# A planned kernel for a hybrid encoder: two-tensor work taken off GpSimd, and twelve planning rounds in place of one

## The chip, the cores and the metric

The kernel runs on one core of one Trainium2 chip. The time is that of the device, in microseconds (us), for the whole program from the inputs in the chip's memory to the output there. Five engines work side by side, each in the order in which its own instructions stand: TensorE (PE, matrix products; PEld is its loading of weights), VectorE (DVE), ScalarE (ACT), GpSimd (POOL), and SyncE (SP), which here only issues transfers. They wait for each other by semaphores.

## The reference

Four residual layers on a sequence of 256 tokens of 1024 numbers; layers 0 and 3 mix tokens by RWKV-7, layer 1 by stick-breaking attention, layer 2 by attention over 64 selected keys. An FFN follows each.

```python
for i in range(DEPTH):                       # DEPTH = 4
    kind, j = i % 3, i // 3
    h = rms_norm(x, norm_mix[i])
    if kind == 0:   y, v_layer = rwkv7_time_mix(h, v_first, ...)
    elif kind == 1: y = stick_breaking_attention(h, sb_w_qkv[j], sb_w_out[j])
    else:           y = dsa_attention(h, ds_w_in[j], ...)
    x = x + y
    x = x + swiglu(rms_norm(x, norm_ffn[i]), ffn_w_gu[i], ffn_w_down[i])

def rms_norm(x, g): return x * rsqrt(mean(x * x) + 1e-6) * g
def swiglu(h, w_gu, w_down):
    g, u = split(h @ w_gu, 2)
    return (silu(g) * u) @ w_down
...
# dsa_attention, for a block of 64 queries
idx = einsum('bqhd,bsd->bqhs', qi_b, ki)
score = einsum('bqh,bqhs->bqs', wi_b, relu(idx))
top_val, top_idx = lax.top_k(where(visible, score, -inf), 64)
p = softmax(q_b . k[top_idx] * 64 ** -0.5)
```

RWKV's recurrence keeps a 64 by 64 state for each of 16 heads and goes through the tokens in order; the kernel does it in four chunks of 64 tokens.

## The kernel before, in words

Everything lies with the 1024 channels on partitions (8 groups of 128) and the 256 tokens along the free axis. Weights come from memory in 397 pieces of 128 x 1024 numbers (tile raw, four slots). Where float32 accuracy is wanted at a faster matmul rate, a piece is split into a rounded part wh (an ACT or DVE copy) and its remainder wl (DVE), three slots each; activations are split the same way (xg, h, yhl, ohl, rhl).

The kernel is not issued as it is written. Each call is recorded (Plan.record) as an operation with its estimated cost and its dependencies, and Plan.schedule then builds one order for each engine: a list scheduler (_schedule) goes through the operations by rank, the length of the longest chain behind them. Some operations may go to either of two engines; the table ALTS lists them, and the scheduler picks. For "any tensor_tensor" the two were DVE and GpSimd. Where it expects PE to have nothing ready or to run too empty, it puts in matmuls of a constant (tile warm_o, two at a time), called warm-ups here.

Three kinds of storage are shared out by the plan: PSUM banks (groups ps with 5 and g with 2), SBUF slots (t with 12, wh, wl, and the big ones by name: SB, QC, PR, s0, s1, s6, s7, xb), and the groups raw and xm, which are given during scheduling in a fixed turn. For the first two kinds, _prepare walked the buffers by their first use in the order in which the program was written, gave each the slot that was last used longest ago in that order, and made every first user of the new buffer wait for all users of the old one. Ranks were computed on those dependencies. The scheduler tries a reserve of free raw slots from 1 to 6 and takes the first with which it gets through.

The parts that the prediction speaks of, by tile names:

- prep_chunk: after each quarter of a residual update (xt), its squares (sq, by ACT) are summed into sqa ("any" tensor_tensor), and xg, the scaled input of the next FFN or attention, is made (ACT and DVE).
- rwkv: kp, rp and vp are the products with plain float32 weights; lora_in, la and lw the small ones; sc the chunk scores (to SB); a triangular inverse goes through memory (scr, xa, xi, scx, XT) and is put together by cmb; then two chains of small products (xu, qu, pS, Y) go through the four chunks for each half of the heads; post makes ysd and yhl of them (two "any" tensor_tensor calls for each pair of heads), and po is the output product.
- dsa: idx are the index scores, sbt holds their weighted sum, from which 8 rounds of max and match_replace pick 64 keys for each query; mk is the mask made of it; vps the value products; then for each of 8 pairs of heads qk, its norm (qss), its rotation (qrot, with one "any" tensor_tensor), the scores z, the softmax (prs), its transpose pT, attn_o, and at the end po.
- ffn: 22 gate, 22 up and 8 down products (gate, up, dn), in split form.

Of the kernel before, what the change touches and what calls it, by code (L numbers as in the profile page):

```python
# [61 lines left out]
class Region:  # L62


    def __init__(self, p0, p1, cols, width):
        self.p0, self.p1 = p0, p1
        cols = np.asarray(cols).ravel()
        self.lo, self.hi = int(cols.min()), int(cols.max()) + 1
        self.mask = None
        if len(cols) < self.hi - self.lo or len(np.unique(cols)) < self.hi - self.lo:  # L70
            self.mask = np.zeros(width, bool)
            self.mask[cols] = True
# [106 lines left out]
class Op:  # L179


    def __init__(self, eng):
        self.eng, self.instrs, self.cost, self.table, self.cols = eng, [], 0.0, None, 0.0
        self.preds, self.succs, self.alts, self.warmer, self.parts = set(), [], {}, False, False
        self.bufs, self.ns = [], 0.0


class Queue:
# [5 lines left out]
    def __getattr__(self, method):  # L194
# [4 lines left out]
          AF.Tanh: "sigmoid_and_others", AF.Silu: "silu_and_others"}  # L199

ALTS = {("any", "copy"): [("scalar", "copy"), ("vector", "tensor_copy")],
        ("any", "tensor_tensor"): [("vector", "tensor_tensor"), ("gpsimd", "tensor_tensor")],
        ("any", "memset"): [("gpsimd", "memset"), ("vector", "memset")]}


# [10 lines left out]
ROW = 3  # L216
GAP = 1100.0
RESERVES = (1, 2, 3, 4, 5, 6)

WAIT = {"tensor": 85.0, "vector": 55.0, "scalar": 40.0, "gpsimd": 40.0, "sync": 0.0}  # L220
FREE = ("raw", "xm")
# [58 lines left out]
class Plan:  # L280
# [95 lines left out]

    def _prepare(self, counts):

        for b in self.bufs:
            if b.ops:  # L380
                b.ops = list(dict.fromkeys(b.ops))
                b.first, b.last = min(o.idx for o in b.ops), max(o.idx for o in b.ops)
        self.grouped, held = {}, {}
        for b in sorted((b for b in self.bufs if b.ops and b.group is not None), key=lambda b: b.first):
            if b.group in FREE:
                self.grouped.setdefault(b.group, []).append(b)
                for o in b.ops:
                    o.bufs.append(b)
                continue
            slots = held.setdefault(b.group, [None] * counts.get(b.group, 1))  # L390
            k = min(range(len(slots)), key=lambda i: -1 if slots[i] is None else slots[i].last)
            old = slots[k]
            if old is not None:
                assert old.last < b.first, (b.name, old.name, b.group)
                for o in b.roots:
                    o.preds |= {q for q, _ in old.writes + old.reads if q is not o}
            slots[k], b.slot = b, f"{b.group}_{k}"
        load, table, now, before = None, None, [], []
        for o in list(self.ops):
            if o.table is None:  # L400
                continue
            if o.table != table:
                table, before, now = o.table, now, []
                load = Op("scalar")
                load.cost, load.table, load.idx = 1290.0, table, o.idx - 0.5
                load.preds |= set(before)
                self.ops.append(load)
            o.preds.add(load)
            now.append(o)
        self.ops.sort(key=lambda o: o.idx)  # L410
        for o in self.ops:
            o.preds.discard(o)
            for q in o.preds:
                assert q.idx < o.idx
                q.succs.append(o)
        for o in reversed(self.ops):
            o.base = o.eng, o.cost
            o.rank = o.cost + max((s.rank + self._lat(o, s) for s in o.succs), default=0.0)

    def _schedule(self, counts, reserve):  # L420
        engines = ("tensor", "vector", "scalar", "gpsimd", "sync")
# [206 lines left out]
        return max(free.values()), sorted(out, key=lambda o: o.start)  # L628

    def schedule(self, counts):  # L630
        self._prepare(counts)
        best = None
        for reserve in RESERVES:
            r = self._schedule(counts, reserve)
            if r is not None:
                best = r
                break
        self.time, self.out = best
        Plan.last = self
        return self.out  # L640

# [1087 lines left out]
```

## Time and profile before

| | |
|---|---|
| three runs | 1474.48, 1473.09, 1474.14 us; median 1474.14 |
| profiled execution | 1473.95 us, of which the span from first to last instruction is 1472.2 |
| granted TensorE clock | 0.999 over the span |
| ACT, POOL busy | 718.3 us, 61.3 us |
| weights and other transfers | 224.55 MB, 151 GB/s read and written over the span |

The profile gives, for an engine and a kind of operation, the number of instructions, their busy time, and the mean of one, and what ended the idle time in front of them. An operation is named by what it writes and reads, without buffer numbers. Nearly all instructions are issued by one line of the planner (L661), so tiles tell them apart and lines do not. A plain float32 matmul of the program stands in the trace as two rows. The duration of a matmul reaches from issue to result, and matmuls overlap: what one costs is the distance from one start to the next. The stages, by time: RWKV 13 to 225 us, FFN to 406, stick-breaking to 530, FFN to 711, sparse attention to 882, FFN to 1064, RWKV to 1285, FFN to the end.

### The profile page before, as it was taken

The page shows a single profiled execution, that of the slowest core. Times are in us where ns is not written, and L with a number is a line of the kernel's source. Part 1 is how long each engine was busy: PE and PEld are TensorE (multiplying, and loading weights), DVE is VectorE, ACT ScalarE, POOL GpSimd, SP SyncE. Part 2 cuts the span into 40 slices and gives each one's busy share as a digit, 9 for nine tenths or more (in the row PEclk, how much of TensorE's full clock was granted, in tenths as well). Part 3 has the DMA queues.
Part 4 walks back from the last instruction along what each step waited for, and adds up shares of the span by engine and source line. Part 5 has one row for each costly group of instructions (what it writes and reads, how often), then busy time and mean ns, then how long its engine had stood idle before and what let it go on. Part 6 is the DMA issues. An engine that isn't in the chain of part 4 may idle for free.

```text
span 1472.2 us, 26233 instructions
## 1 busy us (share of the span) xinstructions
PE 1447.0 (98%) x10434; PEld 1228.1 (83%) x10434; DVE 1107.1 (75%) x2026; ACT 718.3 (49%) x1348; POOL 61.3 (4%) x57
## 2 busy tenths in 40 slices
PE   9999999999999999999999989999999999999998
PEld 6788788888888888888977868888877877888887
DVE  7297478998566779986789978986474884789864
ACT  2344665444447655444546755444325256654442
POOL 0000010000000010000100010000100001200000
PEclk9999999999999999999999999999999999999999
DMA  7234135655554445555634445555523430455653
GB/s 254 91 107 144 36 101 172 194 183 194 175 183 136 130 158 186 198 187 181 192 113 130 129 144 172 186 193 183 197 93 108 129 101 18 130 175 182 196 188 132
DMA packets 77803, 224.55 MB, mean 153 GB/s; under 512 B 23536, under 2 KB 23792, under 8 KB 77424
## 3 DMA queue, kind: packets, MB, share of 16 engines
q1 hardware_dynamic: 77680, 222.87, 46.4%
q8 instruction: 82, 1.34, 0.4%
q14 instruction: 41, 0.34, 0.1%
HBM read 219.70 MB, written 3.15 MB: 151 GB/s over the span
## 4 chain that ended last, share of the span: by engine, by line
PE 86%; DVE 9%; ACT 2%; DMA 2%; issue 1%; SPq 0%; POOL 0%; DVEq 0%
PE up L661 17%; PE dn L661 16%; PE gate L661 16%; PE qk L661 5%; PE po L661 4%; PE kp L661 4%; PE rp L661 4%; PE vps L661 3%; PE z L661 2%; DVE wl L661 2%; PE vp L661 2%; PE warm_o L1564 1%; PE Y L661 1%; PE sc L661 1%; DVE xg L661 1%
## 5 line engine op out<-in xcount | busy, mean ns | idle before, releaser
L661 ACT CAST wh<-raw 128x1024 fp32r<-128x1024 f32 x317 | 329.7, 1050 | 401.8 <-PE dn L661 130.2
L661 DVE TENSOR_TENSOR wl<-raw,wh 128x1024 fp32r<-128x1024 f32 x349 | 420.3, 1222 | 70.0 <-ACT wh L661 58.5
L661 PE MATMUL gate<-xg,wh 128*128 128x512 f32 x704 | 259.9, 398 | 3.9 <-DVE xg L661 2.1
L661 PE MATMUL up<-xg,wh 128*128 128x512 f32 x704 | 259.9, 397 | 0.0
L661 PE MATMUL dn<-h,wh 128*128 128x512 f32 x704 | 247.6, 394 | 0.0
L661 PE MATMUL dn<-h,wl 128*128 128x256 f32 x704 | 197.5, 280 | 0.0
L661 PE MATMUL gate<-xg,wl 128*128 128x256 f32 x704 | 197.2, 280 | 0.0
L661 PE MATMUL up<-xg,wl 128*128 128x256 f32 x704 | 197.2, 280 | 0.0
L661 PEld LDWEIGHTS gate<-xg,wh 128*128 128x128 f32 x704 | 132.2, 188 | 38.1 <-DVE xg L661 3.4
L661 PEld LDWEIGHTS up<-xg,wh 128*128 128x128 f32 x704 | 132.2, 188 | 31.1
L661 PEld LDWEIGHTS dn<-h,wh 128*128 128x128 f32 x704 | 132.4, 188 | 30.8
L661 PEld LDWEIGHTS up<-xg,wl 128*128 128x128 f32 x704 | 132.8, 189 | 0.2
L661 PEld LDWEIGHTS gate<-xg,wl 128*128 128x128 f32 x704 | 132.8, 189 | 0.1
L661 PEld LDWEIGHTS dn<-h,wl 128*128 128x128 f32 x704 | 132.4, 188 | 0.0
L661 PE MATMUL qk<-xg,wh 128*128 128x256 f32 (+1 forms) x384 | 95.0, 326 | 0.1
L661 PE MATMUL qk<-xg,wl 128*128 128x256 f32 x256 | 72.0, 281 | 0.4 <-DVE wl L661 0.4
L661 PEld LDWEIGHTS qk<-xg,wh 128*128 128x128 f32 x384 | 64.2, 189 | 7.8 <-issue 1.4
L661 PE MATMUL kp<-pre,raw 128*128 128x256 f32 x256 | 59.9, 386 | 1.7 <-DVE pre L661 1.7
L661 DVE TENSOR_TENSOR gus<-gus,rstd 128x512 f32<-128x512 f32 x88 | 59.8, 687 | 1.2
L661 PE MATMUL vp<-xv,raw 128*128 128x256 f32 x256 | 59.0, 385 | 0.9 <-DVE vf L661 0.9
L661 PE MATMUL rp<-xr,raw 128*128 128x256 f32 x256 | 58.7, 382 | 0.0
L661 PEld LDWEIGHTS kp<-pre,raw 128*128 128x128 f32 x256 | 47.3, 190 | 13.3 <-issue 4.0
(292 smaller groups left out, 2355.5 us busy)
## 6 DMA issues: line engine op xcount, KB each, us to landing
raw<-in_wts_dram SPq DMA_DIRECT2D x397, 512.0 KB, 3.6
lora<-in_lora_dram SPq DMA_DIRECT2D x2, 1536.0 KB, 9.2
lg<-in_lora_dram SPq DMA_DIRECT2D x4, 512.0 KB, 5.4
xt<-in_xT_dram SPq DMA_DIRECT2D x4, 256.0 KB, 4.0
lora<-in_lora_dram SPq DMA_DIRECT2D x2, 512.0 KB, 5.6
xi<-in_id_dram SPq DMA_DIRECT2D x2, 512.0 KB, 8.0
scr<-SB SPq DMA_DIRECT2D x8, 128.0 KB, 3.4
xa<-scr SPq DMA_DIRECT2D x2, 512.0 KB, 3.3
```

The costliest lines, as they stand in the source:

```text
L661: getattr(getattr(nc, o.eng), method)(*map(real, args), **{k: real(a) for k, a in kw.items()})
L1564: lambda: [nc.tensor.matmul(wo[:, :S], wx[:, :P], wx, start=True, stop=True) for _ in range(WARMERS)])
```

## The change

Two things are changed in the planner; the computation is the same.

First, "any tensor_tensor" has only DVE left. POOL keeps some memsets and copies.

Second, slots are given anew in each of twelve rounds. _prepare now only collects the buffers and keeps each operation's own dependencies (needs). _place takes an order, sorts the buffers by their first use in that order, gives each the slot whose last user ends earliest in it, adds the waits that follow, and recomputes the ranks; the turn of raw and xm is sorted by the same order. schedule begins with the written order, schedules, and hands the outcome (without warm-ups) to the next round as its order. The round that ends earliest by the plan's own estimate is kept, with its engines, forms and slots.

```diff
 ALTS = {("any", "copy"): [("scalar", "copy"), ("vector", "tensor_copy")],
-        ("any", "tensor_tensor"): [("vector", "tensor_tensor"), ("gpsimd", "tensor_tensor")],
+        ("any", "tensor_tensor"): [("vector", "tensor_tensor")],
         ("any", "memset"): [("gpsimd", "memset"), ("vector", "memset")]}
...
+ROUNDS = 12
...
-        self.grouped, held = {}, {}
-        for b in sorted((b for b in self.bufs if b.ops and b.group is not None), key=lambda b: b.first):
...
-            slots = held.setdefault(b.group, [None] * counts.get(b.group, 1))
-            k = min(range(len(slots)), key=lambda i: -1 if slots[i] is None else slots[i].last)
-            old = slots[k]
-            if old is not None:
-                assert old.last < b.first, (b.name, old.name, b.group)
-                for o in b.roots:
-                    o.preds |= {q for q, _ in old.writes + old.reads if q is not o}
-            slots[k], b.slot = b, f"{b.group}_{k}"
...
+    def _place(self, counts, order):
+
+        at = {o: i for i, o in enumerate(order)}
+        for o in self.ops:
+            o.preds, o.succs = set(o.needs), []
+        for g, bufs in self.grouped.items():
+            bufs.sort(key=lambda b: min(at[o] for o in b.ops))
+        for g, bufs in self.placed.items():
+            slots = [None] * counts.get(g, 1)
+            for b in sorted(bufs, key=lambda b: min(at[o] for o in b.ops)):
+                k = min(range(len(slots)), key=lambda i: -1.0 if slots[i] is None else max(o.end for o in slots[i].ops))
+                old = slots[k]
+                if old is not None:
+                    for o in b.roots:
+                        o.preds |= {q for q, _ in old.writes + old.reads if q is not o}
+                slots[k], b.slot = b, f"{g}_{k}"
...
     def schedule(self, counts):
+
+
         self._prepare(counts)
-        best = None
-        for reserve in RESERVES:
-            r = self._schedule(counts, reserve)
-            if r is not None:
-                best = r
-                break
-        self.time, self.out = best
+        order, best = self.ops, None
+        for o in order:
+            o.start, o.end = o.idx, o.idx + 0.5
+        for _ in range(ROUNDS):
+            self._place(counts, order)
+            for reserve in RESERVES:
+                r = self._schedule(counts, reserve)
+                if r is not None:
+                    break
+            if best is None or r[0] < best[0]:
+                best = r + ([(o.eng, o.cost, o.instrs, o.start, o.end) for o in r[1]], [b.slot for b in self.bufs])
+            order = [o for o in r[1] if not o.warmer]
+        self.time, self.out = best[:2]
...
```

In the built programs the change shows as follows. PE has the same matmuls in another order, and 246 warm-ups in place of 294. POOL's two-tensor operations, 40 of them, stand on DVE. A few operations that may go to ACT or DVE have changed sides (so wh: 29 on DVE in place of 32). SP issues the same transfers, the weight pieces in the order in which the plan uses them.

More of the change, by code (lines that the diff above doesn't have):

```diff
@@ L184, in __init__ @@
         self.preds, self.succs, self.alts, self.warmer, self.parts = set(), [], {}, False, False
-        self.bufs, self.ns = [], 0.0
+        self.bufs, self.ns, self.end = [], 0.0, 0.0
 class Queue:
@@ L377, in _prepare @@
     def _prepare(self, counts):
+        self.grouped, self.placed = {}, {}
         for b in self.bufs:
@@ L382, in _prepare @@
                 b.first, b.last = min(o.idx for o in b.ops), max(o.idx for o in b.ops)
-        self.grouped, held = {}, {}
-        for b in sorted((b for b in self.bufs if b.ops and b.group is not None), key=lambda b: b.first):
[L385 to L389, printed above, removed]
-            slots = held.setdefault(b.group, [None] * counts.get(b.group, 1))
-            k = min(range(len(slots)), key=lambda i: -1 if slots[i] is None else slots[i].last)
-            old = slots[k]
-            if old is not None:
-                assert old.last < b.first, (b.name, old.name, b.group)
-                for o in b.roots:
-                    o.preds |= {q for q, _ in old.writes + old.reads if q is not o}
-            slots[k], b.slot = b, f"{b.group}_{k}"
+                if b.group in FREE:
+                    self.grouped.setdefault(b.group, []).append(b)
+                    for o in b.ops:
+                        o.bufs.append(b)
+                elif b.group is not None:
+                    self.placed.setdefault(b.group, []).append(b)
         load, table, now, before = None, None, [], []
@@ L412, in _prepare @@
             o.preds.discard(o)
+            o.needs, o.base = frozenset(o.preds), (o.eng, o.cost)
+    def _place(self, counts, order):
[13 more added lines that the diff above has]
+                slots[k], b.slot = b, f"{g}_{k}"
+        for o in self.ops:
+            o.preds.discard(o)
             for q in o.preds:
-                assert q.idx < o.idx
+                assert at[q] < at[o]
                 q.succs.append(o)
-        for o in reversed(self.ops):
-            o.base = o.eng, o.cost
-            o.rank = o.cost + max((s.rank + self._lat(o, s) for s in o.succs), default=0.0)
+        for o in reversed(order):
+            o.rank = o.base[1] + max((s.rank + self._lat(o, s) for s in o.succs), default=0.0)
     def _schedule(self, counts, reserve):
@@ L631, in schedule @@
         self._prepare(counts)
-        best = None
-        for reserve in RESERVES:
-            r = self._schedule(counts, reserve)
-            if r is not None:
-                best = r
-                break
-        self.time, self.out = best
+        order, best = self.ops, None
[11 more added lines that the diff above has]
+        self.time, self.out = best[:2]
+        for o, state in zip(best[1], best[2]):
+            o.eng, o.cost, o.instrs, o.start, o.end = state
+        for b, slot in zip(self.bufs, best[3]):
+            b.slot = slot
         Plan.last = self
```

## The prediction

> **What bounds the kernel now.** I read the page's shares first, then the busy time by stage, then the waits and the timeline of the places that the stages pointed to.
>
> ```profile
> span 1472.2 us, 26233 instructions
> PE 1447.0 (98%) x10434; PEld 1228.1 (83%) x10434; DVE 1107.1 (75%) x2026; ACT 718.3 (49%) x1348; POOL 61.3 (4%) x57
> PEclk9999999999999999999999999999999999999999
> PE 86%; DVE 9%; ACT 2%; DMA 2%; issue 1%; SPq 0%; POOL 0%; DVEq 0%
> ```
>
> TensorE is busy for 98% of the span at a full granted clock, and 86% of the chain that ended last is PE's. So 1472.2 - 1447.0 = 25.2 us of PE idleness is all that an order can gain, plus whatever PE does that is not work: the 294 warm-up matmuls. The busy time by stage says where the idleness lies (columns: us, then busy us of PE, PEld, DVE, ACT, POOL, granted clock, DMA share, GB/s).
>
> ```profile
> 13.00:225.00 212.00, 207.95 (x2088) 167.08 (x2088) 144.23 (x352) 100.71 (x273) 12.82 (x13) 1.00 0.35 113
> 225.00:406.00 181.00, 181.00 (x1032) 157.94 (x1031) 145.63 (x214) 83.75 (x105) 3.67 (x3) 1.00 0.55 183
> 711.00:882.00 171.00, 162.46 (x1172) 139.04 (x1171) 145.43 (x289) 101.39 (x225) 12.42 (x10) 1.00 0.44 140
> 1064.00:1285.00 221.00, 216.11 (x2158) 173.03 (x2155) 151.54 (x383) 105.92 (x280) 11.85 (x11) 1.00 0.32 99
> ```
>
> These are the first RWKV layer (4.05 us idle), an FFN (none), the sparse-attention layer (8.54) and the second RWKV layer (4.89). An FFN has nothing to give: no order makes its matmuls shorter. The three mixers hold 17.5 of the 25.2 us.
>
> **The warm-up matmuls.** The planner writes them where it expects PE to wait, so their number in a built program says how much waiting it sees. Their price is a spacing, not the 273 ns that one takes from issue to result:
>
> ```profile
> 9.21 3.88 PE L1564 MATMUL warm_o<-warm_x 128*128 128x256 bf16 x34
> L1564 PE MATMUL warm_o<-warm_x x294: 272/273/421, 1.2 to 1242.3; 128*128 128x256 bf16 x147
> ```
>
> 34 of them span 3.88 us, so (3.88 - 0.27) / 33 = 0.109 us each. The changed program's instruction list has 246: 90 instead of 96 by the end of the first RWKV layer, 36 instead of 64 in sparse attention, 86 instead of 100 for the second RWKV layer with its start, and 34 the same elsewhere. All other PE instructions are the same in kind and number, only in another order. 48 x 0.109 = **5.2 us** is gone from PE if the waits that they stood for are covered by work; if they are not, nothing is gained here (the far end, 0).
>
> **Sparse attention, its end.** Of those 28, more than all come out of the last heads: 40 warm-ups stood there (8, 6, 22 and 4), and the new list has none behind its last 8, since the products of the output projection (po) and of the last heads stand between the steps of a head. What the warm-ups didn't cover was idle:
>
> ```profile
> 829.00:870.00 41.00, 37.96 (x288) 30.52 (x288) 29.31 (x65) 25.36 (x67) 0.00 (x0) 1.00 0.39 133
> 853.34 0.73 PE L661 MATMUL qss<-rhl,bonesr 128*128 128x512 f32 x2 [0.86 <-ACT prs L661]
> 861.42 2.56 PE L1564 MATMUL warm_o<-warm_x 128*128 128x256 bf16 x22
> 864.99 0.85 PE L661 MATMUL pT<-consts,prs 128*128 128x128 f32 x6 [1.00 <-DVE prs L661]
> ```
>
> 41.00 - 37.96 = 3.0 us, each wait right behind a run of warm-ups or at a softmax step. With work in their place I take 2.0 of it as gained (bounds 0 and 3.0).
>
> **Sparse attention, its middle.** Here the change takes cover away. The selection of keys is one line of DVE work, and the masked scores wait for its end. Before, the value products (vps) stood behind the index scores; now 48 of them stand ahead of the last index scores, and 28 + 8 warm-ups (before 14 + 8) fill part of the hole.
>
> ```profile
> L661 DVE TENSOR_TENSOR wl<-raw,wh 128x1024 fp32r<-128x1024 f32 x349 | 420.3, 1222 | 70.0 <-ACT wh L661 58.5
> 747.00:776.00 29.00, 25.36 (x186) 21.10 (x186) 27.81 (x83) 13.44 (x22) 1.59 (x3) 1.00 0.26 82
> 750.91 1.58 PE L661 MATMUL idx<-ki,sbt 64*128 64x128 f32 x16
> 750.94 4.70 DVE L661 SCALAR_TENSOR_TENSOR sbt<-sbt,wi 128x256 f32<-128x256 f32 x14
> 758.26 0.08 DVE L661 MATCH_VALUE_LOAD sbt<-m,sbt 128x8 f32 x1
> 759.43 0.08 DVE L661 MATCH_VALUE_LOAD sbt<-m,sbt 128x8 f32 x1
> 761.53 0.86 DVE L661 SCALAR_TENSOR_TENSOR qa<-qa,vecs,sbt 128x256 f32<-128x256 f32 x2
> 770.06 0.67 DVE L661 TENSOR_TENSOR qa<-qrot,sbt 128x512 f32<-128x512 f32 x1
> 765.82 0.49 PE L661 MATMUL qrot<-rhl,rotr 128*128 128x512 f32 x1 [1.73 <-DVE rhl L661]
> 773.82 0.35 DVE L661 TENSOR_SCALAR mk<-sbt 128x384 bf16<-128x384 f32 x1
> 415.56 10.98 PE vps L661 x48
> 502.97 5.76 PE po L661 x48
> ```
>
> One round of the selection is 759.43 - 758.26 = 1.17 us, eight are 9.4. The new DVE list has between the last index scores and the mask (mk) 12 weighted sums (4.70 / 14 = 0.336 each, 4.0), the 9.4, four qa scalings (1.7), two weight residuals wl (1.22 each, 2.4), nine 512-wide operations of rhl, qa and qk at 0.67 (6.0) and the mask (0.4): 23.9 us. PE has 120 matmuls of qk in that stretch, at the spacing of po, whose shape is the same (5.76 / 48 = 0.12: 14.4), ten of qss and qrot (at the 0.23 of vps, 2.3), four score matmuls, half of what eight idx ones take (16 trace rows, 1.58: 0.8), and 36 warm-ups (3.9): 21.4. It will wait some 2.5 us. Before, it was idle for 29.00 - 25.36 = 3.64 in the same place. I take no difference (bounds 3.6 gained and 4 lost).
>
> **What moves from POOL to DVE.** Forty two-tensor operations: 18 + 2 sums of squares, 3 + 1 in the rotary steps (all 512 wide) and 16 of the RWKV output (256 wide). On DVE one costs what its like costs there:
>
> ```profile
> L661 DVE TENSOR_TENSOR gus<-gus,rstd 128x512 f32<-128x512 f32 x88 | 59.8, 687 | 1.2
> L661 DVE TENSOR_TENSOR ysd<-Y,ysd 128x256 f32<-128x256 f32 x16 | 6.5, 419 | 6.6 <-ACT ysd L661 6.6
> L661 POOL TENSOR_TENSOR sqa<-sqa,sq 128x512 f32<-128x512 f32 x18 | 28.7, 1595 | 555.3 <-ACT sq L661 490.8 <-issue 64.5
> L661 DVE SCALAR_TENSOR_TENSOR xg<-xt,vecs,xg 128x256 fp32r<-128x256 f32 x48 | 34.7, 759 | 0.0
> L661 DVE SCALAR_TENSOR_TENSOR xg<-xt,vecs,xg x8: 473/480/1522, 522.2 to 530.6; 128x256 fp32r<-128x256 f32 x8
> L661 DVE TENSOR_TENSOR yhl<-ysd,yhl 128x256 fp32r<-128x256 f32 x16 | 8.6, 547 | 2.3 <-ACT yhl L661 2.3
> PEld gate L661 <- DVE xg L661: 3.4, 4, 0.8
> ```
>
> 24 x 0.687 + 16 x 0.419 = 23.2 us more on DVE. But POOL's work was not free for DVE: an xg operation takes 480 ns at the median and up to 1522 beside a POOL sum, and the mean of all 48 is 759, so 48 x 0.279 = 13.4 us of DVE's busy time was waiting for POOL; yhl adds 16 x (0.547 - 0.419) = 2.0. DVE's net load is about +8 us on 1107, and where it falls DVE has slack against PE (145 of 181 us in an FFN). [...]
>
> On PE's path this touches the four passages from a mixer to an FFN, where the first gate products wait for xg in four places of up to 0.8 us (3.4 in all), and the last output heads of RWKV. In the new DVE list one sum stands ahead of the last xt addition there (0.69 later), with a wl and that addition queued behind it on DVE, and the gate products behind those; its square comes from ACT one xt addition earlier, so I see no wait in front of it. The stalled xg that followed is free again (up to 1.0 earlier). In RWKV's output the two operations behind a head's scale become 0.42 each on DVE instead of 0.7 to 1.6 on POOL. I take 1.5 us gained in all (bounds: 4 x 0.69 = 2.8 lost, the 3.4 gained).
>
> **The sum.** The profiled execution took 1473.95 us, 1.75 beside its span; the median of the runs is 1474.14. 1473.95 - 5.2 - 2.0 + 0 - 1.5 = **1465.2**. The unpriced part is where each RWKV layer's instructions, now with other banks and slots and the first weight piece pair issued ahead of the lora piece on SP, wait for each other; its 4.05 + 4.89 = 8.9 us of idleness may fall away or double. I take it unchanged.
>
> **Rivals.** (1) *The waits stay and only the filler goes.* A warm-up that is deleted from a wait which is still there saves nothing. For it speaks that 17.5 us of waiting in the mixers came on top of all warm-ups, so the planner sees too few waits; against it, that in the sparse-attention end real products replace them. Then only the 1.5 remains: 1472.5, no change. (2) *The selection becomes the bound, and the kernel is slower.* The 48 value products are 10.98 us of cover that is gone from behind the index scores. DVE serves its line in order; if the two wl in it come late, the qk products that need them stop as well, and PE waits out the cover that left, 2.5 + 11.0 instead of 2.5, so 1465.2 + 11.0 = 1476.2, and with the 1.5 not gained, 1477.7. It decides from the point where DVE's 23.9 us stretch by more than PE's own waiting hides. For it: DVE is busy for 27.81 of 29.00 us there already. Against it: of the DVE line's 23.9 us, PE has 21.4 of its own. (3) *TensorE's clock drops where warm-ups were taken out.* Before the clock is up, a warm-up takes more:
>
> ```profile
> 1.19 5.73 PE L1564 MATMUL warm_o<-warm_x 128*128 128x256 bf16 x30 [1.19 <-DVE eps_rms L661]
> ```
>
> (5.73 - 0.27) / 29 = 0.188 us against 0.109, so a cold stretch costs about 0.7 of its length again. If 10 us of the two RWKV chains, where 20 warm-ups go, ran cold, that is +7: 1472, no change. The clock row, all nines, says that nothing was near that before. [...] (4) *RWKV's own waits go too*: with 8.9 us less, 1456.
>
> **How the numbers follow.** Forecast 0.63, rival 4 0.08 (both faster), rival 1 0.13, rival 3 0.04 (both no change, which is what within 0.2%, 2.9 us, can't be told from), rival 2 0.12 (slower). So faster 0.71, same 0.17, slower 0.12. Predicted: 1465 us. Low end: the sum with 3.0, 3.6 and 3.4 gained is 1473.95 - 5.2 - 10.0 = 1458.8, and half of RWKV's idleness less gives 1454. High end: 1477, which leaves out rival 2's far end alone. The forecast's own range is 1458 to 1471.
>
> **What would show it.** Warm-ups x246; PE idle in the sparse-attention stage near 6 us instead of 8.5, and its length near 166 us; no wait over 0.5 us at its last heads; waits for the mask or rhl of about 2.5 us in its middle; xg's mean near 480 ns with no 1500 among them; POOL under 15 us busy; FFN stages still 181 us; granted clock 1.00 throughout. Wrong would be: a wait on mk, rhl or wl in the middle of 6 us or more (rival 2), stages of unchanged length with fewer warm-ups in them (rival 1), a clock under 0.99 in an RWKV stage (rival 3), or RWKV's stages growing by more than their warm-ups shrink.

## The result, and the profile after

The changed kernel takes 1455.15 us (median of four runs, 1454.46 to 1456.18) against 1473.66 for the kernel before beside it: a ratio of 0.987 (0.9856 to 0.9885), 18.5 us less. The forecast was 1465; the range of 1454 to 1477 holds the time, but the gain is twice what was forecast, and the total is that of rival 4 (1456), by luck, as shown below. The profiled execution took 1456.18 us with a span of 1454.4, so 17.8 us are to be accounted for against the 1472.2 of before.

The changed kernel's page, its shares:

```profile
span 1454.4 us, 26104 instructions
PE 1435.8 (99%) x10386; PEld 1222.8 (84%) x10386; DVE 1101.0 (76%) x2063; ACT 720.9 (50%) x1351; POOL 8.9 (1%) x17
PE 90%; DVE 6%; ACT 1%; issue 1%; DMA 1%; SPq 0%; DVEq 0%; POOL 0%
```

PE's idleness is 1454.4 - 1435.8 = 18.6 us, 6.6 less than before; its busy time is 11.2 us less, with the same real matmuls. So the larger part of the gain came out of time that the page had called busy. The warm-ups are a part of that; their rows, before and after:

```profile
L1564 PE MATMUL warm_o<-warm_x 128*128 128x256 bf16 x294 | 44.0, 285 | 1.2 <-DVE eps_rms L661 1.2
L1589 PE MATMUL warm_o<-warm_x 128*128 128x256 bf16 x246 | 36.2, 286 | 1.2 <-DVE eps_rms L686 1.2
```

They are 7.8 us less. These rows overlap their neighbours at both ends, so 48 spacings of 0.109 us, 5.2, are the low estimate. Between 3.4 and 6.0 us of the 11.2 came out of matmuls that do work.

The mixers, cut from the first working matmul of one stage to that of the next (every cut lies 0.24 us ahead of it). First the kernel before (columns as in the prediction: us; busy of PE, PEld, DVE, ACT, POOL; clock; DMA):

```profile
13.73:219.17 205.44, 202.88 (x2062) 163.24 (x2062) 137.92 (x343) 96.89 (x266) 10.31 (x11) 1.00 0.35 111
712.25:875.94 163.69, 156.02 (x1139) 133.89 (x1137) 138.60 (x281) 97.43 (x217) 9.68 (x8) 1.00 0.43 138
1070.68:1280.52 209.84, 206.84 (x2096) 165.87 (x2096) 143.96 (x370) 99.27 (x268) 9.95 (x10) 1.00 0.31 93
```

And after:

```profile
13.65:215.71 202.06, 201.01 (x2054) 161.40 (x2055) 137.57 (x352) 97.28 (x267) 2.74 (x2) 1.00 0.35 112
707.24:862.51 155.27, 150.53 (x1110) 131.11 (x1108) 128.23 (x275) 103.14 (x230) 0.29 (x2) 1.00 0.45 145
1056.93:1264.02 207.09, 204.40 (x2081) 164.76 (x2082) 144.64 (x382) 98.76 (x266) 1.13 (x1) 0.99 0.31 94
```

Sparse attention is 8.4 us shorter, the RWKV layers 3.4 and 2.7 (2.75 from unrounded starts). The idle time of PE in the three goes from 2.56, 7.67 and 3.00 to 1.05, 4.74 and 2.69: 4.75 us less, where the stages shrank by 14.55. All stages, by the same cuts (gate/up and down are the FFN's two parts), for the changed kernel and the experiments that matter most, each against the kernel before:

| stage | before, us | after | e2: one round | e3: POOL allowed | e8: slots only | e7: banks only |
|---|---|---|---|---|---|---|
| RWKV 1 | 205.44 | -3.39 | -0.06 | -2.10 | -1.74 | +1.47 |
| gate/up | 123.91 | -0.65 | -0.61 | -0.01 | -0.61 | -0.61 |
| stick-breaking | 118.48 | -0.24 | -0.45 | +0.09 | -0.45 | -0.24 |
| gate/up | 123.18 | -0.66 | -0.70 | -0.01 | -0.70 | -0.66 |
| sparse attention | 163.68 | -8.41 | -3.91 | -7.31 | -3.96 | -9.96 |
| gate/up | 123.23 | -0.11 | -0.65 | +0.55 | -0.66 | -0.66 |
| RWKV 2 | 209.83 | -2.75 | -1.51 | +0.40 | -1.56 | +4.48 |
| gate/up | 123.37 | -1.19 | -0.67 | -0.18 | -0.76 | -0.75 |
| start, the four downs, norm | | -0.36 | -0.14 | +0.10 | +0.05 | +0.35 |

In the row RWKV 2 the changed kernel, e3 and e7 ran in part at a lower clock (0.99, 0.98 and 0.97 over that stage), so it does not show their order alone. A second profile of the changed kernel gives -3.64, -8.39 and -1.81 for the three mixers.

The changed kernel's groups of instructions, and its warm-ups by their tile:

```profile
L686 PE MATMUL gate<-xg,wh 128*128 128x512 f32 x704 | 259.0, 397 | 1.6 <-DVE xt L686 1.6
L686 DVE SCALAR_TENSOR_TENSOR xg<-xt,vecs,xg 128x256 fp32r<-128x256 f32 x48 | 21.2, 478 | 0.0
L686 DVE TENSOR_TENSOR sqa<-sqa,sq 128x512 f32<-128x512 f32 x18 | 12.3, 683 | 0.0
```

```profile
L1589 PE MATMUL warm_o<-warm_x x246: 272/273/421, 1.2 to 1230.4; 128*128 128x256 bf16 x123
```

xg's mean is 478 ns (759 before, with sums on POOL); what idle time is left ahead of the gate products (1.6 us) is put down to xt, none to xg.

The middle of sparse attention, on PE's timeline after:

```profile
767.78 1.58 PE L686 MATMUL idx<-ki,sbt 64*128 64x128 f32 x16
...
778.89 3.23 PE L1589 MATMUL warm_o<-warm_x 128*128 128x256 bf16 x28
783.22 0.51 PE L686 MATMUL qrot<-rhl,rotr 128*128 128x512 f32 x1 [0.87 <-DVE rhl L686]
790.33 1.05 PE L1589 MATMUL warm_o<-warm_x 128*128 128x256 bf16 x8
792.62 0.50 PE L686 MATMUL qss<-rhl,bonesr 128*128 128x512 f32 x1 [1.01 <-DVE rhl L686]
793.05 0.93 PE L686 MATMUL z<-qk 64*128 64x128 f32 x8
```

All 36 warm-ups of the stage are these 28 + 8, and the waits behind them are 1.88 us. The masked scores z come right after the second of them: the selection of keys did not become the bound.

### The profile page after: what moved, and what is told of

Its sections match the earlier page's. It is cut to its first block, busy times and chain, and to the rows that moved or that the text cites. A ratio compares the mean times of both kernels' runs of the same rounds, so it can differ in the third digit from the quotient of the medians.

```text
span 1454.4 us, 26104 instructions
## 1 busy us (share of the span) xinstructions
PE 1435.8 (99%) x10386; PEld 1222.8 (84%) x10386; DVE 1101.0 (76%) x2063; ACT 720.9 (50%) x1351; POOL 8.9 (1%) x17
## 4 chain that ended last, share of the span: by engine, by line
PE 90%; DVE 6%; ACT 1%; issue 1%; DMA 1%; SPq 0%; DVEq 0%; POOL 0%
PE up L686 17%; PE gate L686 17%; PE dn L686 17%; PE qk L686 5%; PE po L686 5%; PE vp L686 4%; PE rp L686 4%; PE kp L686 4%; PE vps L686 3%; PE z L686 2%; PE Y L686 1%; PE sc L686 1%; DVE wl L686 1%; PE warm_o L1589 1%; PE qi L686 1%
## 5 line engine op out<-in xcount | busy, mean ns | idle before, releaser
L686 ACT CAST wh<-raw 128x1024 fp32r<-128x1024 f32 x320 | 333.9, 1050 | 412.1 <-PE dn L686 130.3
L686 PE MATMUL kp<-pre,raw 128*128 128x256 f32 x256 | 63.4, 389 | 1.9 <-DVE pre L686 1.7
```

The source lines that it names most:

```text
L686: getattr(getattr(nc, o.eng), method)(*map(real, args), **{k: real(a) for k, a in kw.items()})
```

## The experiments

The differences of the stages above tell two theories apart. The lock theory: POOL's two-tensor work blocked DVE, and its removal is the gain. The order theory: the gain is from slots given by use, round after round.

Each ratio below is against the kernel before beside it. The intervals of e4, e5, e6, e8, e11 and e12 overlap with that of the changed kernel (0.9856 to 0.9885), so between those kernels the stages of the profiled executions carry the argument, not the totals.

**e1: the order of before, POOL's 40 operations on DVE at their places.**

```diff
+eng = "vector" if o.eng == "gpsimd" and method == "tensor_tensor" else o.eng
-getattr(getattr(nc, o.eng), method)(...)
+getattr(getattr(nc, eng), method)(...)
```

> The order of the kernel before, every bank, slot and warm-up as it was; only the 40 two-tensor operations that stood on POOL are issued on DVE at the same place. Lock theory (half of the 18.5 us and more came from DVE no longer waiting for POOL): 1474 - 9 = 1465 us or less, and the four passages to an FFN give 2 to 3 us of it. Order theory (the gain came from the slots given anew, twelve times): 1471 to 1475 us, since DVE's busy time changes by only some 8 us and PE's order is fixed.

Measured: 1471.53 us (12 runs), ratio 0.998 (0.9959 to 0.9994). In the profile the four passages into gate/up gain 0.43, 0.40, 0.37 and 0.51; sparse attention gains 1.41; the first RWKV layer loses 1.40. That profiled execution is 3.6 us above its own median, with a granted clock of 0.66 from 1170 to 1180 us, so the +3.13 of its second RWKV layer is not charged to the edit. Freed from POOL but kept in the old order, the kernel gains some 3.5 us (0.9 to 6.0 by the interval).

**e2: the change with one planning round. e3: the change with POOL allowed again for two-tensor work.**

```diff
-ROUNDS = 12
+ROUNDS = 1
```

> The changed kernel with one planning round in place of twelve: no two-tensor work on POOL, slots by the written order, 332 warm-ups. Lock theory: near 1463 us. Order theory: no better than before; 38 warm-ups more than before are 4.1 us at 0.109, so 1474 to 1478 us. If warm-ups stand for nothing but waits that would be there anyway, it comes out like e1.

```diff
-        ("any", "tensor_tensor"): [("vector", "tensor_tensor")],
+        ("any", "tensor_tensor"): [("vector", "tensor_tensor"), ("gpsimd", "tensor_tensor")],
```

> Twelve rounds with POOL still allowed for two-tensor work: 46 of them on POOL, 236 warm-ups (10 fewer than the changed kernel). Order theory: as fast as the changed kernel or up to 1 us faster, 1454 to 1456 us. Lock theory: DVE is blocked by POOL for some 20 us again, and 1462 to 1466 us.

Measured: e2 1465.38, ratio 0.993 (0.9904 to 0.9949); e3 1464.60, ratio 0.992 (0.9897 to 0.9942). The spans are 8.7 and 8.5 us shorter than before, 17.2 together, against 17.8 for the whole change: two halves that add, and neither theory alone. By their totals both lie at or near what the lock theory had put down for them (1463, and 1462 to 1466); that theory fails at e1, which it put at 1465 or less, and at the places. The places differ: e2 has every passage into gate/up and 3.9 us of sparse attention, e3 none of the passages and 7.3 us of sparse attention. e2 has 332 warm-ups, 38 more than before, and is faster all the same: its first RWKV layer has 80 in place of 62 and is as long (-0.06).

**e4: the changed kernel's order, its 22 sums of squares on POOL.**

```diff
+eng = "gpsimd" if method == "tensor_tensor" and args[0].buf.name in ("sqa", "sq") \
+    and args[1].buf.name in ("sqa", "sq") else o.eng
```

> The changed kernel's order with 22 sums of squares (sqa and sq) put back on POOL at the same place. It prices the lock alone at the passages to an FFN. Lock theory: the four passages lose the 0.7 to 1.2 us each that they gained, and the total is 1458 to 1461 us. Order theory: within 1.5 us of the changed kernel, 1455 to 1456.5 us.

Measured: 1460.87, ratio 0.990 (0.9871 to 0.9921); the span is 1459.7, so the 22 sums cost 5.3 us. Its groups:

```profile
L687 DVE SCALAR_TENSOR_TENSOR xg<-xt,vecs,xg 128x256 fp32r<-128x256 f32 x48 | 34.7, 758 | 0.0
L687 POOL TENSOR_TENSOR sqa<-sqa,sq 128x512 f32<-128x512 f32 x18 | 29.4, 1631 | 841.6 <-ACT sq L687 477.2 <-issue 364.4
```

And its waits of the weight loads of PE:

```profile
PEld gate L687 <- DVE xg L687: 3.4, 4, 0.8
```

These are the kernel before's 759 ns and 3.4 us back again. Against the changed kernel the four gate/up parts grow by 0.64, 0.66, 0.83 and 0.65, 2.8 us; another 1.24 is the start, where POOL takes 2.61 us for two sums that DVE does in 1.49 (PE's ss waits 1.4 us for them, 0.55 in the changed kernel), and the rest small pieces of the mixers. By what POOL holds DVE up, no run shows: the rows show how long xg takes with a sum on POOL beside it and without. Nor does it pay here to hand two-tensor work back to GpSimd, with VectorE busy for 76% of the changed kernel's span: e3 has 46 operations on POOL, and its span is 9.3 us longer.

**e5 and e6: the changed kernel's order with one and with three matmuls for each warm-up pair, 123 and 369 in place of 246.**

```diff
-for _ in range(WARMERS)
+for _ in range(WARMERS - 1)        # e6: WARMERS + 1
```

> The changed kernel's order with one matmul in place of two wherever a warm-up stands: 123 warm-ups of 246. 50 of those left out lie at the start and before the second RWKV layer, where PE waits for the norm anyhow. Price theory (each of the other 73 costs its 0.109 us): 8 us less, 1447 us. Filler theory (they stand in waits that stay): 1453 to 1456 us with more PE idle. Clock theory: over 1456 us with a granted clock under 0.995.

> The same order with three matmuls in place of two at each warm-up: 369. Price theory: 8 us more, 1463 us, since 73 of the 123 added ones lie in the mixers at 0.109. Filler theory: 1455 to 1458 us, with PE idle shrinking by what the warm-ups grow.

Measured: e5 1462.22, ratio 0.990 (0.9864 to 0.9928); e6 1463.60, ratio 0.990 (0.9873 to 0.9933). The spans of their profiled executions are 4.0 and 6.7 us longer than the changed kernel's. Windows of e5, sparse attention and ten microseconds of the second RWKV layer:

```profile
708.09:863.38 155.29, 149.89 (x1092) 130.73 (x1091) 128.26 (x275) 103.20 (x230) 0.29 (x2) 0.99 0.46 144
...
1208.00:1218.00 10.00, 10.00 (x175) 7.91 (x174) 3.45 (x13) 4.71 (x18) 0.00 (x0) 0.52 0.08 32
```

and of e6, sparse attention and the first RWKV layer:

```profile
711.33:866.60 155.27, 151.93 (x1128) 132.78 (x1126) 128.25 (x275) 103.18 (x230) 0.29 (x2) 1.00 0.46 144
...
15.57:219.77 204.20, 203.52 (x2086) 164.23 (x2085) 137.13 (x350) 97.41 (x267) 2.90 (x2) 1.00 0.35 106
```

With 18, 36 and 54 warm-ups the stage has the same length, 155.29, 155.27 and 155.27: there a warm-up only turns idle time into busy time (5.40, 4.74, 3.34 us idle). In the first RWKV layer, 28 more make 204.20 - 202.06 = 2.14 us, 0.076 each. Neither place pays the 0.109 of the forecast. e6's total is the price theory's 1463, but by luck: the three mixers hold 3.8 of its 6.7 us (2.14, 0.00 and, for the second RWKV layer, 208.78 - 207.09 = 1.69), where that theory had 8, and most of the rest lies at the start and ahead of the second RWKV layer, which it took as free. The filler theory's total (1455 to 1458) missed as well. e5 came out as the clock theory said: what it saves in filler it loses to the clock, 0.52 in the ten microseconds shown, 0.993 over its span; its first RWKV layer begins 3.0 us later, and its second takes 3.05 us longer.

**e7 and e8: twelve rounds, but only the PSUM banks, or only the SBUF slots, given by the use in the order ahead.** The other kind is given by the order in which the program was written.

```diff
+            use = g in ("ps", "g")              # e8: g not in ("ps", "g")
-            for b in sorted(bufs, key=lambda b: min(at[o] for o in b.ops)):
-                k = min(..., key=lambda i: ... max(o.end for o in slots[i].ops))
+            for b in sorted(bufs, key=lambda b: min(at[o] for o in b.ops) if use else b.first):
+                k = min(..., key=lambda i: ... max(o.end for o in slots[i].ops) if use else slots[i].last)
```

> Twelve rounds in which only the PSUM banks (groups ps and g) are given by the use in the order ahead; SBUF slots stay as in one round. 270 warm-ups. If the gain of the rounds (10 us between one round, 1465.4, and the changed kernel, 1455.2) comes from banks: 1455 to 1459 us, with the sparse-attention stage at 155 to 157. If from SBUF slots: 1462 to 1466 us.

> The other half: only SBUF slots are given by use, the banks stay as in one round. 304 warm-ups. If the gain comes from banks: 1462 to 1466 us, sparse attention near 160. If from slots: 1455 to 1459 us.

Measured: e7 1467.02 (11 runs, 1461.66 to 1473.23), ratio 0.993 (0.9902 to 0.9952); e8 1463.90, ratio 0.990 (0.9872 to 0.9931). e7's total lies above both ranges put down for it; its runs go from 1461.66 us at a granted clock of 0.999 to 1473.23 at 0.991. The stages say more than the totals: sparse attention is 153.73 us in e7 and 159.72 in e8, against 159.78 with one round. So the rounds' gain there is the banks' alone. The last heads on PE's timeline show how. First e8:

```profile
838.35 0.87 PE L687 MATMUL attn_o<-sbt 128*64 128x256 f32 x8
...
853.33 0.93 PE L687 MATMUL z<-qk 64*128 64x128 f32 x8
854.18 0.50 PE L687 MATMUL z<-mk,identb 128*128 128x384 bf16 x2
854.52 2.56 PE L1590 MATMUL warm_o<-warm_x 128*128 128x256 bf16 x22
858.08 0.85 PE L687 MATMUL pT<-consts,prs 128*128 128x128 f32 x6 [1.00 <-DVE prs L687]
859.17 1.25 PE L687 MATMUL attn_o<-sbt 128*64 128x256 f32 x8 [0.24 <-ACT sbt L687]
860.35 0.61 PE L1590 MATMUL warm_o<-warm_x 128*128 128x256 bf16 x4
```

and the changed kernel, its output products (po) between the lines shown:

```profile
838.31 0.93 PE L686 MATMUL z<-qk 64*128 64x128 f32 x8 [0.23 <-DVE qk L686]
...
840.63 0.93 PE L686 MATMUL z<-qk 64*128 64x128 f32 x8
...
844.03 1.52 PE L686 MATMUL attn_o<-sbt 128*64 128x256 f32 x16
...
847.00 0.82 PE L686 MATMUL pT<-consts,prs 128*128 128x128 f32 x6
...
848.36 0.82 PE L686 MATMUL pT<-consts,prs 128*128 128x128 f32 x6
...
851.24 1.52 PE L686 MATMUL attn_o<-sbt 128*64 128x256 f32 x16
```

In e8 the last pair of heads goes through scores, softmax, transposes and values by itself, with 22 warm-ups and a wait where the softmax runs. In the changed kernel the scores of two pairs stand 2.3 us apart, their transposes 1.4 apart, and their value products in one run of 16, with po between: the softmax of one hides behind the work of the other. The rows also show waiting that no idle column of PE counts: the last pair's eight attn_o take 1.25 us in e8, those of an earlier pair 0.87, and sixteen of the changed kernel 1.52. Behind the 1.25 stand, in e8:

```profile
858.64 0.86 ACT L687 COPY sbt<-pT 128x384 f32<-128x384 f32 x2 [0.29 <-PE pT L687]
859.55 0.62 PEld L687 LDWEIGHTS attn_o<-sbt 128*64 128x64 f32 x6 [0.19 <-ACT sbt L687]
```

Six of the eight weight loads wait for ACT's copy, which ends at 859.50. PE counts as busy meanwhile, and the chain that is late shows as the longer row, 1.25 us for 0.87, instead of as idle time.

In RWKV neither kind alone gives the 3.39 us of the first layer (e8 1.74, e7 a loss of 1.47), so there both seem to be needed; which slots they are, and by what waits they act, no run tells.

**e11 and e12: can the changed kernel be beaten?** e11 has one matmul in place of two at the 25 warm-up places of the first RWKV layer's chains; e12 takes the eighth round's order in place of the kept one. A repeat of the changed kernel, with the same runs of the kernel before, gave 1455.42 and 0.986 (0.9837 to 0.9888):

> The changed kernel unchanged, on the chip of the next two, to set them side by side: 0.985 to 0.989 of the kernel before by every theory.

The edit of e11, and then of e12:

```diff
+for _ in range(1 if 35 <= next(nth) < 60 else WARMERS)
```

> The changed kernel with one matmul in place of two at the 25 warm-ups of the first RWKV layer's chains only; start and second layer keep theirs. With one matmul at every warm-up (e5) that stage took 2.0 us less and lost no clock, while the start and the second layer lost 3 each. If a warm-up costs 0.07 there as e5 and e6 say: 1.5 to 2 us below the changed kernel of the same chip. If the clock needs them: no gain, with a granted clock under 0.998 in that stage.

```diff
-            if best is None or r[0] < best[0]:
+            if n == 7:
```

> The changed kernel with the order of the eighth round in place of the one that it keeps (the fifth): 240 warm-ups, other banks and slots. If any order that uses banks and slots by the order ahead has the gain: within 4 us of the changed kernel of the same chip. If the gain lies in picking one out of twelve: 8 us or more above it.

Measured: e11 1459.67, ratio 0.990 (0.986 to 0.9931), in two groups: three runs of 1454.6 to 1455.1 at a granted clock of 0.998 to 0.999, three of 1464.3 to 1466.4 at 0.989 to 0.990. e12 1460.17, ratio 0.991 (0.9872 to 0.9939), with 1456.65 to 1457.4 at a clock of 0.998 and 1463 to 1469 at 0.988 to 0.994. e11's profile is one of the cold executions. Its windows:

```profile
152.08:155.49 3.41, 3.16 (x70) 2.05 (x63) 3.18 (x7) 1.73 (x7) 0.00 (x0) 1.00 0.17 65
155.49:182.80 27.31, 27.31 (x411) 20.56 (x412) 4.91 (x19) 11.75 (x44) 0.00 (x0) 0.50 0.07 22
182.80:186.20 3.40, 3.40 (x75) 2.89 (x72) 1.50 (x5) 2.81 (x11) 0.00 (x0) 1.00 0.02 5
```

and the same stretch of the changed kernel, with the one in which its own clock fell:

```profile
152.08:155.49 3.41, 3.41 (x71) 2.30 (x68) 3.07 (x7) 1.73 (x7) 0.00 (x0) 1.00 0.09 34
155.49:158.90 3.41, 3.41 (x80) 2.44 (x80) 0.28 (x2) 2.44 (x9) 0.00 (x0) 1.00 0.48 159
...
1159.35:1162.76 3.41, 3.34 (x26) 2.39 (x25) 3.09 (x13) 2.54 (x8) 0.00 (x0) 1.00 0.85 296
1162.76:1166.17 3.41, 3.41 (x8) 2.75 (x9) 3.34 (x13) 3.39 (x10) 0.00 (x0) 0.50 0.05 17
```

Where the clock stayed up, the leaner chain gains nothing; where it did not, it loses some 10 us. (The expectation took from e5 that the stage loses no clock; e5's own first RWKV layer stood at 0.99.) e12's executions at full clock lie 1.2 to 2.0 us above the repeat's 1455.42, within the 4 us put down for an order that uses banks and slots by the order ahead: the gain does not hang on the one order that was picked. Neither version beats the changed kernel.

## Why the prediction was right in sign and too small

**The step that failed is the premise**, that the 25.2 us of PE idleness is all that an order can gain, plus the warm-ups. The span fell by 17.8 us: idleness by 6.6, where 2.0 + 1.5 was forecast, and PE's busy time by 11.2, where only the 5.2 of the warm-ups was. Matmuls that do work were put at nothing and gave 3.4 to 6.0 us; the attn_o rows of e8 show one such wait inside the busy time; and the waits in RWKV were put at nothing as well.

**The warm-up term (-5.2) held as busy time, but it is no price.** It asked that work stand in the places of the warm-ups, and in sparse attention it does. The warm-ups' own busy time there (the second figure), before and after:

```profile
712.25:875.94 163.69, 8.17 (x64) 1.00 0.43 138
707.24:862.51 155.27, 4.28 (x36) 1.00 0.45 145
```

3.9 us are gone, where 28 x 0.109 = 3.05 was forecast. But a count times a spacing holds under that condition alone. The warm-ups that are left cost nothing in sparse attention (e5, e6) and some 0.07 us each in the first RWKV layer (28 fewer save 1.97 in e5, 28 more cost 2.14 in e6). And the count does not size a gain: e2 has 38 more than before and is 8.7 us shorter in span. Rival 1 named this, that a filler taken out of a wait which stays saves nothing; it was wrong that the waits stay.

**Sparse attention.** The two terms for it (28 x 0.109 = 3.05 and 2.0) made 5.05; measured 8.41. Its middle was taken at no difference, and that fits: its idle time went from 3.64 us to 0.87 + 1.01 = 1.88, and 14 more warm-ups (36 for 22, 14 x 0.109 = 1.5) take up the difference. So rival 2 fell: about 2.5 us of waiting was forecast, and a wait of 6 or more would have shown that rival. The gain is at the heads and the end, where the mechanism was right (products of the last heads and of po between the steps of a head) and the size too small. PE's idle time at the heads and the end fell by 1.3 us, from 4.00 (776 to 876) to 2.68 (793 to 862.5), where 2.0 was taken; so what the sum lacked lay in the busy time. In the code, e2 has 3.91 of the 8.41 with the banks of the written order, and the banks bring the rest, as e7 and e8 show; the prediction had only the new order to go by. "No wait over 0.5 at the last heads" held for the last two pairs; at earlier ones two of 0.57 and 0.87 are left, on PE's timeline after:

```profile
822.93 0.55 PE L686 MATMUL pT<-consts,prs 128*128 128x128 f32 x3 [0.57 <-ACT prs L686]
...
826.23 0.73 PE L686 MATMUL qss<-rhl,bonesr 128*128 128x512 f32 x2 [0.87 <-ACT prs L686]
```

**The POOL-to-DVE term (-1.5).** Right in kind, and inside its bounds (+2.8 to -3.4): the four gate/up parts gain 0.65, 0.66, 0.11 and 1.19, 2.6 in all, and e4 gives 2.8 back. xg's mean (478 ns, forecast near 480) and POOL's 8.9 us (forecast under 15) hold. The size was taken too low by 1.1 us. DVE's load was misjudged with it: it was to rise by some 8 us, and DVE's busy time fell from 1107.1 to 1101.0; in e1, in the old order, it fell to 1105.8 although 40 operations came on top. So POOL had slowed more of DVE's work than the xg and yhl rows that the prediction counted. The down products of the FFNs, 63.88 and 63.62 us in the first two before and after, are unchanged, as forecast.

**RWKV, "taken unchanged".** Only its 20 warm-ups were priced, 2.2 us. Measured: 3.39 + 2.75 = 6.1, the second with a granted clock of 0.83 from 1160 to 1170 us, so rather more. So 3.9 us of the shortfall lie here, the part that was left unpriced and that rival 4 covered with 8.9. Most of it came out of busy time (idleness fell by 1.5 and 0.3). So rival 4's total is luck: it let 8.9 us of RWKV's idleness go, and 1.8 went. What shortens the RWKV layers stays open.

**The sum of the misses**: sparse attention 3.4, RWKV 3.9, passages 1.1, stick-breaking, downs and start 0.6: 9.0 of the 17.8 - 8.7.

**The clock (rival 3)** did not decide in the changed kernel: 0.998, with 0.99 in the second RWKV stage, where "1.00 throughout" missed the 3.41 us shown above. But the fear was sound: e5, e7, e11 and e12 lost several us to it. The kernel before is not free of it either: 5 of its 44 executions beside the experiments took 1485 to 1486 us at 0.989 to 0.990. The price was near: in e11, 0.01 of 1460 us less granted clock is 29 us at half clock; it costs some 11 us, 0.6 of the 18 us that the work takes warm, where 0.7 was forecast. That figure came from the warm-ups of the first microseconds. The clock record of the kernel before begins at 5.9 us, at 1.00; their lengths are 421 ns at the median up to 5.4 us and 273 from 5.6 to 6.7 us, and those of e11's 25, from 152 to 184 us, go from 273 to 421 across its stretch at 0.50.

## What to carry to other kernels

Read a wait as a place, not as a column: the filler, the idle time and the lengthened matmuls around it went together here when work took its place (3.9, 2.9 and 1.6 of sparse attention's 8.4 us), and the order gained more there than the 7.7 us of idle time. When banks or slots are handed out by the written order, look in the timeline for chains that run one after the other although they are independent; here new banks alone were worth 6 us in a stage of 160. Before moving work to GpSimd, compare VectorE's two-input operations with and without it beside them (478 and 758 ns here), and count the slowed ones as its price.

## What the runs showed of the hardware

The granted clock had two levels in these traces, 1.00 and 0.50, and in two falls that the windows above show PE had been busy for most of the time. In e11 it fell behind 3.41 us in which PE was busy for 3.16 by the profile, with 70 small matmuls; the changed kernel, with 71 and 3.41 busy in the same place, kept it. But its own clock fell at 1162.76 us, behind 3.34 busy of 3.41, so the busy time of a profile did not tell when the clock fell, and no run shows what does. Once down it stayed down in e11 for 27.31 us in which PE was busy without a gap, and came back by itself. By the clock records of the traces, cold stretches lasted 3.41 us (the changed kernel, e4), 6.83 (its repeat, e1, e3), 10.24 (e12, and the one of e5 shown above), 13.65 (e7) and 27.31 (e11): one, two, three, four and eight times 3.41, but for rounding. One program can run cold for long or hardly at all, from run to run: e11's runs differ by 11 us, at clocks of 0.989 to 0.999, and e7's go from 1461.7 at a clock of 0.999 to 1473.2 at 0.991. So warm-ups that save nothing in any one wait still had a use here as insurance: with 123 (e5) all six executions stood at 0.987 to 0.993, with 246 all ten at 0.998 or more, with 369 (e6) all six as well. Their number alone does not decide it, since the kernel before with 294 and e7 with 270 fall at times (to 0.989 and 0.991). And a median of few runs of such a program says little without its clocks.
